# One decoder block on one core: a hand-written order around the MoE routing gets more dummy matmuls ahead, fewer within, an index list earlier and four low parts ahead of other work

## The chip, the cores and the metric

The kernel runs on one core of one Trainium2 chip. The metric is the device time of one execution in microseconds (us); the median of several runs counts. The engines are PE (TensorE: matmuls and transposes), DVE (VectorE), ACT (ScalarE), POOL (GpSimd) and SP (SyncE, which issues most loads). Each engine works through its own instructions strictly in the order in which the program lists them; an instruction whose input is late holds up all that stands behind it on its engine. Matmuls whose type is float32 run here in passes: a matmul of float32 with float32 shows as two records in the trace.

## The reference

A post-norm decoder block with 512 tokens of 1024 channels. The part that matters here comes after attention and the linear recurrence:

```python
x = layer_norm(ALPHA * x + (1 + gt_m) * mix, ln1_g, ln1_b)
u = layer_norm(x) * (1 + sc_f) + sh_f
# routing: top-1 of 4 groups, then top-2 of the 4 experts in that group
grp_prob = softmax(u @ w_grp + b_grp)
grp_w, grp_idx = top_k(grp_prob, 1)
top_w, top_idx = top_k(softmax(sel_logits), 2)
top_w = top_w / sum(top_w) * grp_w
# 16 experts of width 512
h = silu(u @ w_e_gate[e]) * (u @ w_e_up[e])
y = y + comb[:, e] * (h @ w_e_down[e])
x = layer_norm(ALPHA * x + (1 + gt_f) * y, ln2_g, ln2_b)
```

## The kernel before

**Tiles.** The 512 tokens are four tiles of 128 (t = 0 to 3). `TAIL` is a list of closures written out by hand; called one after the other, they set the order of PE, ACT, DVE and POOL from the end of attention to the start of the experts. Behind the list the program order of PE and SP stays as it is written, while ACT, DVE and POOL are interleaved by a scheduler at build time.

**Per token tile.** `L[t][0]` to `L[t][4]` are the steps of the output layer norm (the x of tile t is made on DVE at L945; L957, L978, L984, L994 and L998 follow; the last step stores u to DRAM at L999). `RT[t]` transposes x (PE, L1008), `RE[t]` copies the transposes (ACT, L1013), `RL[t]` is the 8 matmuls of the router (PE, L1034) and `RN[t]` turns them into logits (DVE, L1040 and L1041). `SX[t]` scales x on ACT (L1018) and stores it to `x2d` from ACT's DMA queue (L1019).

**The choice.** `R[0]` to `R[4]` choose group, first and second expert on DVE (from L1191), join the choices in the mask `mkb` (L1212) and count positions with small matmuls on PE (L1215 and L1217, then L1225 and L1228). `K(n)` puts n dummy matmuls of the identity on PE (L1123), whose result nobody reads. `KR(name, n)` puts n dummies on PE that read the mask `em` or the first choice (L1131; the first choice is called `oh1` in the code and `e1o` in the trace), so they start when it is there.

**Gathering expert 0's tokens.** `FO` makes one-hot masks, `FM(t)` multiplies them with u of tile t (PE, L1551, 16 records for one tile) and `FX` splits the sums into a high part `x0h` (ACT, L97) and a low part `x0l` (DVE, L98). `IX[p]` makes the list of token numbers for slot block p: one-hot on DVE (L1379 or L1370), 8 matmuls on PE (L1317), a copy on DVE (L1321). `OR, PT, SP_, PP` sort the experts by load; `PP` leaves the positions on DVE (L1571, L1573). `WM` makes the routing weights `wm` from DVE (L1233 to L1252) and two small ACT steps (L1235, L1241).

**Expert weights.** A weight tile `er` (512 KB, loaded by SP at L819) is split into a high part `whi` (ACT, L811) and a low part `wlo` (DVE, L812; the low part of each second tile of four goes to POOL). `pre_split(g)` does that for gate tile g of expert 0. `whi` and `wlo` have four buffers, so a fifth split waits until PE has finished the first tile. A half (gate, up or down) of an expert is four tiles with six matmuls each (L101 whi x high, L102 wlo x high, L103 whi x low). Right behind the list comes expert 0's gate half, then `IX[2]`, then the transposes of `wm` on PE (L1289, with a copy `sT` on ACT at L1291), then expert 0's up half, then the gathered rows of expert 1 (L1409) and its gate half. Later slot blocks hold 64 tokens each; the last ones are the L1418 matmuls (gate and up, in float32 straight from `er`), L1502 and L1400 (transposes), and a down half as above.

Of the kernel before, what the change touches and what calls it, by code (L numbers as in the profile page):

```python
# [19 lines left out]
S = 512  # L20
# [27 lines left out]
def block_kernel(ctx, tc, x, c, w_ada, b_ada, w_in, b_f, conv_w, conv_b, w_rg, b_rg, w_ig, b_ig,  # L48
# [1816 lines left out]
```

## Time and profile before

| what | value |
|---|---|
| median of 3 runs | 655.67 us (652.84, 655.67, 656.31) |
| the profiled execution's own time | 654.58 us |
| its span, first to last instruction | 652.8 us |
| busy: PE, DVE, ACT, POOL | 92%, 69%, 49%, 28% |
| chain that ended last: PE, DMA, DVE, ACT | 62%, 18%, 10%, 5% |
| mean granted TensorE clock | 0.97 |

The profiled execution took 654.58 us, 1.8 us more than its span. PE is busy nearly all the time, so a stretch of the profile in which PE stands idle, or runs at a granted clock under 1, is where a change in order can act. A granted clock of 1 is 2.4 GHz, one of 0.5 is 1.2 GHz; shares in between are windows in which both occurred.

### The profile page before, as it was taken

The page shows a single profiled execution, that of the slowest core. Times are in us where ns is not written, and L with a number is a line of the kernel's source. Part 1 is how long each engine was busy: PE and PEld are TensorE (multiplying, and loading weights), DVE is VectorE, ACT ScalarE, POOL GpSimd, SP SyncE. Part 2 cuts the span into 40 slices and gives each one's busy share as a digit, 9 for nine tenths or more (in the row PEclk, how much of TensorE's full clock was granted, in tenths as well). Part 3 has the DMA queues.
Part 4 walks back from the last instruction along what each step waited for, and adds up shares of the span by engine and source line. Part 5 has one row for each costly group of instructions (what it writes and reads, how often), then busy time and mean ns, then how long its engine had stood idle before and what let it go on. Part 6 is the DMA issues. An engine that isn't in the chain of part 4 may idle for free.

```text
span 652.8 us, 10217 instructions
## 1 busy us (share of the span) xinstructions
PE 600.1 (92%) x3537; PEld 440.2 (67%) x3537; DVE 453.3 (69%) x740; ACT 322.3 (49%) x512; POOL 180.0 (28%) x186
## 2 busy tenths in 40 slices
PE   4798999999999999989899999999999899999990
PEld 0455877777886888879677776676667577766550
DVE  6757869845744677787798576938686785895264
ACT  0344797344436364644577454445545464753150
POOL 8800002100000000142155353435354343743000
PEclk9899999999999999997899999999999899999996
DMA  9996136996347305375799979799989999999523
GB/s 311 340 266 201 36 117 196 283 276 199 115 166 285 113 4 191 110 278 197 234 332 380 389 233 349 271 328 350 359 285 346 367 377 363 370 385 368 151 104 124
DMA packets 90862, 165.65 MB, mean 254 GB/s; under 512 B 9351, under 2 KB 29943, under 8 KB 90808
## 3 DMA queue, kind: packets, MB, share of 16 engines
q1 hardware_dynamic: 84080, 150.06, 66.2%
q0 software_dynamic: 5024, 10.70, 6.3%
q10 hardware_dynamic: 1704, 4.21, 1.8%
q8 instruction: 29, 0.48, 0.3%
q14 instruction: 25, 0.20, 0.1%
HBM read 156.58 MB, written 12.39 MB: 259 GB/s over the span
## 4 chain that ended last, share of the span: by engine, by line
PE 62%; DMA 18%; DVE 10%; ACT 5%; issue 3%; ACTq 0%; POOL 0%; SPq 0%; POOLq 0%; DVEq 0%
PE ps L101 12%; PE ps L102 12%; PE ps L103 12%; PE ps L1418 7%; DMA er<-in_w_e_up_dram 6%; DMA er<-in_w_e_down_dram 4%; DMA er<-in_w_e_gate_dram 4%; DVE wlo L812 3%; PE ps L1434 2%; DMA wa<-in_w_ada_dram 2%; PE ps L290 2%; DMA wi<-in_w_in_dram 1%; PE ps L318 1%; ACT pr L861 1%; PE ps L883 1%
## 5 line engine op out<-in xcount | busy, mean ns | idle before, releaser
L812 DVE TENSOR_TENSOR wlo<-er,whi 128x1024 fp32r<-128x1024 f32 x91 | 143.9, 1600 | 28.8 <-ACT whi L811 27.1
L811 ACT CAST whi<-er 128x1024 fp32r<-128x1024 f32 x120 | 125.3, 1049 | 73.7 <-PE ps L103 67.0
L812 POOL TENSOR_TENSOR wlo<-er,whi 128x1024 fp32r<-128x1024 f32 x29 | 74.8, 2579 | 76.8 <-ACT whi L811 76.6
L101 PE MATMUL ps<-uh,whi 128*128 128x512 f32 x160 | 64.4, 403 | 0.0
L102 PE MATMUL ps<-wlo,xth 128*128 128x512 f32 x144 | 58.1, 403 | 5.1 <-POOL wlo L812 4.1
L103 PE MATMUL ps<-uh,wlo 128*128 128x512 f32 x160 | 62.6, 392 | 0.0
L102 PE MATMUL ps<-ul,whi 128*128 128x512 f32 x160 | 62.5, 390 | 0.0
L101 PE MATMUL ps<-whi,xth 128*128 128x512 f32 x144 | 58.9, 409 | 0.0
L1418 PE MATMUL ps<-er,xT 128*64 128x256 f32 x512 | 58.8, 382 | 0.0
L103 PE MATMUL ps<-whi,xtl 128*128 128x512 f32 x144 | 57.6, 400 | 1.2 <-DVE xtl L98 1.2
L1418 PEld LDWEIGHTS ps<-er,xT 128*64 128x64 f32 x512 | 35.4, 137 | 19.4 <-issue 1.9
L326 POOL TENSOR_TENSOR rA<-rA,nhalf 128x1 f32<-128x1 f32 x4 | 2.2, 549 | 157.0 <-DVE rA L917 157.0
L101 PEld LDWEIGHTS ps<-uh,whi 128*128 128x128 f32 x160 | 30.1, 188 | 11.9 <-issue 3.9
L358 DVE TENSOR_TENSOR wlo<-wi,whi 128x1024 fp32r<-128x1024 f32 x20 | 25.5, 1275 | 16.9 <-ACT whi L357 16.9
L102 PEld LDWEIGHTS ps<-wlo,xth 128*128 128x128 f32 x144 | 27.4, 190 | 12.7 <-POOL wlo L812 5.8
L357 ACT CAST whi<-wi 128x1024 fp32r<-128x1024 f32 x20 | 21.0, 1048 | 29.0 <-DMA wi<-in_w_in_dram 20.6
L102 PE MATMUL ps<-wlo,hth 128*128 128x512 f32 x80 | 32.6, 407 | 2.6 <-DVE wlo L812 2.6
L103 PEld LDWEIGHTS ps<-uh,wlo 128*128 128x128 f32 x160 | 30.0, 188 | 6.9 <-DVE wlo L358 0.5
L102 PEld LDWEIGHTS ps<-ul,whi 128*128 128x128 f32 x160 | 30.1, 188 | 6.5 <-issue 0.5
L101 PE MATMUL ps<-whi,hth 128*128 128x512 f32 x80 | 33.0, 412 | 0.0
L103 PEld LDWEIGHTS ps<-whi,xtl 128*128 128x128 f32 x144 | 27.5, 191 | 7.9 <-DVE xtl L98 1.6
L103 PE MATMUL ps<-whi,htl 128*128 128x512 f32 x80 | 32.2, 403 | 0.0
(414 smaller groups left out, 1248.9 us busy)
## 6 DMA issues: line engine op xcount, KB each, us to landing
er<-in_w_e_gate_dram SPq DMA_DIRECT2D x64, 512.0 KB, 9.6
er<-in_w_e_up_dram SPq DMA_DIRECT2D x64, 512.0 KB, 11.3
er<-in_w_e_down_dram SPq DMA_DIRECT2D x64, 512.0 KB, 10.7
wa<-in_w_ada_dram SPq DMA_DIRECT2D x44, 512.0 KB, 6.2
wi<-in_w_in_dram SPq DMA_DIRECT2D x20, 512.0 KB, 7.3
wo<-in_w_out_dram SPq DMA_DIRECT2D x8, 512.0 KB, 5.1
wa<-in_w_ada_dram ACTq DMA_DIRECT2D x4, 512.0 KB, 12.1
x<-in_x_dram SPq DMA_DIRECT2D x4, 512.0 KB, 6.2
```

Of the source, the lines that this page charges most:

```text
L101: T.matmul(o, l[0], r[0], start=start, stop=False)
L102: T.matmul(o, l[0], r[1], start=False, stop=False)
L103: T.matmul(o, l[1], r[0], start=False, stop=stop)
L290: T.matmul(part_p[j][32 * k:32 * k + 32, :], cb[:, 2 * kh - 2 + k, :], part_q[j][kh - 1 + k // 2][:, k % 2, :], start=kh == 1, stop=kh == 3)
L318: T.matmul(p[:, b:b + 1], part[:, b * 128:(b + 1) * 128], s4 if sel_ is None else sel_, start=True, stop=True)
L357: A.copy(hl[0], r)
L358: V.tensor_sub(hl[1], r, hl[0].bitcast(F32))
L811: A.copy(hl[0], r)
L812: (eng or V).tensor_sub(hl[1], r, hl[0].bitcast(F32))
L861: A.activation(pr[j][:, n, :], lg_[j][:, n, :], AF.Exp, bias=nmx[:, j, n:n + 1], accum_out=ss[:, j, n:n + 1])
L1418: T.matmul(p[64 * h:64 * h + 64, :], xT[:, k, :], ws[w0 + k // 2][:, k % 2, h * 256:(h + 1) * 256], start=k == 0, stop=k == 7)
L1434: T.matmul(py[64 * h:64 * h + 64, :], hT[:, k % 2, (k // 2) * 64:(k // 2) * 64 + 64], ws[8 + k][:, h * 512:(h + 1) * 512], start=k == 0, s ...
```

## The change

Only the list `TAIL` is edited, at its end. Eight dummies are put in front of `RT[0]`; the dummies inside the choice go from 5 and 5 to 3 and 2; `IX[1]` moves from behind `FX` to a place before `FM(0)`; `pre_split(1)`, `(2)` and `(3)` follow `FX` directly, and `WM`, `SX[1]` and `SX[0]` come behind them.

```diff
-        ..., L[0][0], RT[0], RL[1], L[1][2], RE[0], RN[2], L[1][3], L[0][1], RL[0], L[0][2], K(10), SX[3], RN[1], L[0][3], SX[2], RN[0], ahead(3), R[0], KR("em", 5), R[1], KR("oh1", 5), R[2], R[3], FO, L[2][4], R[4], FM(3), IX[0], OR, FM(2), L[1][4], PT, SP_, FM(1), L[0][4], PP, FM(0), pre_split(0), FX, IX[1], pre_split(1), SX[1], SX[0], WM, pre_split(2), pre_split(3),
+        ..., L[0][0], K(8), RT[0], RL[1], L[1][2], RE[0], RN[2], L[1][3], L[0][1], RL[0], L[0][2], K(10), SX[3], RN[1], L[0][3], SX[2], RN[0], ahead(3), R[0], KR("em", 3), R[1], KR("oh1", 2), R[2], R[3], FO, L[2][4], R[4], FM(3), IX[0], OR, FM(2), L[1][4], PT, SP_, FM(1), L[0][4], PP, IX[1], FM(0), pre_split(0), FX, pre_split(1), pre_split(2), pre_split(3), WM, SX[1], SX[0],
```

On DVE, before, the end of the routing weights (L1252, `wm`) stands ahead of the low parts of expert 0's third and fourth gate tile and of all of its up tiles (`wlo_3238` and `wlo_3242` are those gate tiles, `wlo_3299`, `wlo_3319` and `wlo_3329` are up tiles 0, 2 and 3):

```order
L1249 TENSOR_TENSOR wm_3232<-e1o_3047,wk_3228 128x64
L1251 TENSOR_TENSOR w_665_3234<-e2o_3064,wk_3229 128x64
L1252 TENSOR_TENSOR wm_3232<-wm_3232,w_665_3234 128x64
L812 TENSOR_TENSOR wlo_3238<-er_2324,whi_3237 128x1024
L812 TENSOR_TENSOR wlo_3242<-er_2326,whi_3241 128x1024
L812 TENSOR_TENSOR wlo_3299<-er_2328,whi_3298 128x1024
L812 TENSOR_TENSOR wlo_3319<-er_2739,whi_3318 128x1024
L1321 TENSOR_SCALAR c_3283<-ps_3273 128x1
L812 TENSOR_TENSOR wlo_3329<-er_2741,whi_3328 128x1024
```

In the changed kernel the last rows up to `wm` on DVE are these (`wlo_3323` and `wlo_3333` are the low parts of up tiles 2 and 3; the low parts of the gate tiles and of up tile 0 stand ahead of these rows):

```order
L812 TENSOR_TENSOR wlo_3323<-er_2739,whi_3322 128x1024
L1243 TENSOR_SCALAR den_3233<-dd_3230 128x4
L1321 TENSOR_SCALAR c_3287<-ps_3277 128x1
L1244 TENSOR_TENSOR den_3233<-den_3233,gw_3228 128x4
L1350 CAST ix_3286<-c_3287 128x1
L1351 SCALAR_TENSOR_TENSOR ix_3286<-c_3287,half 128x1
L1246 RECIPROCAL wk_3236<-den_3233 128x4
L1247 TENSOR_TENSOR wk_3237<-wk_3236,dd_3230 128x4
L1249 TENSOR_TENSOR wm_3240<-e1o_3054,wk_3236 128x64
L1251 TENSOR_TENSOR w_670_3242<-e2o_3068,wk_3237 128x64
L812 TENSOR_TENSOR wlo_3333<-er_2741,whi_3332 128x1024
L1252 TENSOR_TENSOR wm_3240<-wm_3240,w_670_3242 128x64
```

The finished weights now stand behind the low part of up tile 3.

On ACT, before, the two stores of x stand behind the cast of gate tile 1 (`whi_3208`), ahead of the other casts:

```order
L811 CAST whi_3208<-er_2322 128x1024
L1018 ACTIVATE xt_1731<-xt_1731 128x1024
L1019 DMA x2d<-xt_1731 128x1024
L1018 ACTIVATE xt_1730<-xt_1730 128x1024
L1019 DMA x2d<-xt_1730 128x1024
L1235 ACTIVATE gx_3218<-gd_3216 128x16
L1241 ACTIVATE dd_3222<-dd_3222 128x4
L811 CAST whi_3237<-er_2324 128x1024
```

In the changed kernel the stretch of ACT that follows the casts of gate tiles 1 to 3 reads as follows (`whi_3302`, `whi_3312`, `whi_3322`, `whi_3332` are up tiles 0 to 3, `sT_3299` the copy of the transposed weights):

```order
L811 CAST whi_3302<-er_2328 128x1024
L811 CAST whi_3312<-er_2737 128x1024
L1235 ACTIVATE gx_3226<-gd_3224 128x16
L811 CAST whi_3322<-er_2739 128x1024
L1241 ACTIVATE dd_3230<-dd_3230 128x4
L1018 ACTIVATE xt_1731<-xt_1731 128x1024
L811 CAST whi_3332<-er_2741 128x1024
L1019 DMA x2d<-xt_1731 128x1024
L1018 ACTIVATE xt_1730<-xt_1730 128x1024
L1291 COPY sT_3299<-ps_3294 16x512
L1019 DMA x2d<-xt_1730 128x1024
```

Both stores, and the two ACT steps of the weights, now stand behind casts of up tiles, and the second store behind `sT`.

Near the end of the kernel the scheduler's interleaving comes out differently too. On ACT, before, the casts of the last down half (`whi_6123` to `whi_6153`, tiles 0 to 3) stand like this around the split of its input (`hth`), the silu of the next block (`sg`) and a copy of transposes (`xT`):

```order
L811 CAST whi_6123<-er_5845 128x1024
L811 CAST whi_6133<-er_5847 128x1024
L811 CAST whi_6143<-er_5849 128x1024
L97 CAST hth_6089<-ps_6084 128x512
L811 CAST whi_6153<-er_5851 128x1024
L1489 ACTIVATE sg_6169<-ps_6067 128x256
L1401 COPY xT_6110<-ps_6111 128x512
```

And in the changed kernel (`whi_6127` to `whi_6157` are the same four tiles):

```order
L97 CAST hth_6093<-ps_6088 128x512
L1489 ACTIVATE sg_6173<-ps_6071 128x256
L811 CAST whi_6127<-er_5849 128x1024
L1401 COPY xT_6114<-ps_6115 128x512
L811 CAST whi_6137<-er_5851 128x1024
L811 CAST whi_6147<-er_5853 128x1024
L811 CAST whi_6157<-er_5855 128x1024
```

Three of the four casts have moved behind `xT`. DVE's low parts of these tiles moved likewise, behind `htl` (L98) and `sg` (L1490).

## Rows read from the trace of the kernel before

**Rows 1.** Chain that ended last, end of the kernel: start, us, engine or transfer.
```profile
609.28 5.15 DMA x2d<-y,ix
```

**Rows 2.** Busy time by windows: window, length, busy us, PEclk, DMA share, GB/s.
```profile
295.00:300.00 5.00, 5.00 (x25) 5.00 (x25) 4.82 (x13) 3.83 (x7) 2.15 (x4) 0.50 0.49 161
320.00:325.00 5.00, 4.94 (x21) 3.69 (x21) 3.31 (x15) 3.41 (x6) 1.70 (x1) 0.66 0.58 190
375.00:425.00 50.00, 48.83 (x299) 33.04 (x299) 39.14 (x43) 24.95 (x29) 22.80 (x12) 1.00 0.83 284
```

**Rows 3.** Timeline of PE, routing: start, us, instruction [idle before <-releaser].
```profile
292.50 1.72 PE L1008 MATMUL ps<-ident,xt 128*128 128x128 f32 x8 [2.19 <-DVE xt L945]
294.01 6.85 PE L1034 MATMUL ps<-wr,yT 128*128 128x20 f32 x32
300.70 3.82 PE L1123 MATMUL ps<-ident 128*128 128x128 f32 x20
304.45 1.31 PE L1131 MATMUL ps<-ident,em 128*64 128x128 f32 x10
...
306.78 0.21 PE L1215 MATMUL ps<-mkb,utrib 128*128 128x16 bf16 x2
...
316.01 2.05 PE L1551 MATMUL ps<-oh,u 128*128 128x128 f32 x16
320.06 0.35 PE L1317 MATMUL ps<-cidx,oh 128*128 128x1 bf16 x8 [2.00 <-DVE oh L1379]
```

**Rows 4.** Timeline of DVE, routing.
```profile
298.68 1.41 DVE L994 SCALAR_TENSOR_TENSOR u<-xt,nmu,scf 128x512 f32<-128x512 f32 x2
300.90 0.24 DVE L1040 SCALAR_TENSOR_TENSOR lg<-ps,rs,b1w 128x20 f32<-128x20 f32 x1 [0.81 <-PE ps L1034]
...
305.64 0.22 DVE L1212 TENSOR_TENSOR mkb<-e1o,e2o 128x64 bf16<-128x64 f32 x1
...
316.12 0.21 DVE L1571 CAST posb<-ps 128x56 bf16<-128x56 f32 x1 [1.48 <-PE ps L1297]
...
319.32 0.68 DVE L1379 TENSOR_TENSOR oh<-iota1b,posb 128x512 bf16<-128x512 bf16 x1
```

**Rows 5.** Timeline of PE, expert 0 and the start of expert 1.
```profile
326.19 0.50 PE L102 MATMUL ps<-wlo,x0h 128*128 128x512 f32 x1 [1.04 <-DVE wlo L812]
...
328.62 0.40 PE L103 MATMUL ps<-whi,x0l 128*128 128x512 f32 x1
...
329.08 0.60 PE L1289 MATMUL ps<-ident,wm 128*16 128x128 f32 x4
...
339.38 0.50 PE L103 MATMUL ps<-whi,xtl 128*128 128x512 f32 x1 [1.20 <-DVE xtl L98]
```

**Rows 6.** Timeline of DVE, the same stretch.
```profile
324.77 0.22 DVE L1252 TENSOR_TENSOR wm<-wm,w 128x64 f32<-128x64 f32 x1
...
328.75 2.99 DVE L812 TENSOR_TENSOR wlo<-er,whi 128x1024 fp32r<-128x1024 f32 x1 [0.34 <-ACT whi L811]
...
331.74 1.21 DVE L812 TENSOR_TENSOR wlo<-er,whi 128x1024 fp32r<-128x1024 f32 x1
```

**Rows 7.** Timeline of POOL, the same stretch.
```profile
327.52 3.14 POOL L812 TENSOR_TENSOR wlo<-er,whi 128x1024 fp32r<-128x1024 f32 x1 [4.73 <-ACT whi L811]
```

**Rows 8.** Timeline of ACT, the same stretch.
```profile
322.08 0.81 ACTq L1019 DMA_DIRECT2D x2d<-xt  x1
...
329.06 1.05 ACT L811 CAST whi<-er 128x1024 fp32r<-128x1024 f32 x1 [0.34 <-PE ps L103]
```

**Rows 9.** Waits of SP's DMA queue: total us, times, longest us.
```profile
SPq L819 <- DMA x2d<-xt: 18.1, 4, 8.7
```

**Rows 10.** Timeline of ACT, last down half.
```profile
592.66 1.05 ACT L811 CAST whi<-er 128x1024 fp32r<-128x1024 f32 x1 [0.30 <-PE ps L103]
...
602.47 0.59 ACT L1401 COPY xT<-ps 128x512 f32<-128x512 f32 x1 [2.42 <-PE ps L1400]
```

**Rows 11.** Timeline of PE, last down half.
```profile
607.82 0.40 PE L103 MATMUL ps<-whi,htl 128*128 128x512 f32 x1
```

More of the change, by code (lines that the diff above doesn't have):

```diff
@@ L42, in TAIL @@
     return [
-        AL, AL, pj(1, 0), AC, AC, AL, AL, pj(1, 1), AC, AC, T[0], S[1], N[1], AU[6], pj(2, 0), LW["L"], AL, GW("L", 0, V), GW("L", 1, V), FW["L"][0], pj(2, 1), AL, T[1], PV[0], S[2], AU[7], N[2], AC, AC, FW["L"][1], GW("L", 2, V), AL, pj(3, 0), AU[8], FW["L"][2], GW("L", 3, V), AL, pj(3, 1), AC, AC, AU[9], open_e1, T[2], S[3], N[3], PV[1], S[4], FW["L"][3], AL, AL, AL, AL, PV[2], T[3], N[4], RW[0], lo(0, 1), AC, AC, PV[3], LW["A"], scsh_rows, FR[0], FR[1], XA[0], XA[2], lo(0, 0), AC, AC, GW("A", 0, V), lo(1, 0), FR[2], le(0, 0), le(0, 1), XA[1], S[5], T[4], N[5], GW("A", 1, V), S[6], lo(2, 1), PV[4], RW[1], FR[3], FR[4], lo(2, 0), GW("A", 2, V), GW("A", 3, V), le(1, 0), AU[10], lo(1, 1), FR[5], le(1, 1), XA[3], S[7], T[5], N[6], SS[3], le(2, 1), S[8], PV[5], lo(3, 0), T[6], N[7], le(2, 0), AU[11], lo(3, 1), FW["A"][0], FW["A"][1], FW["A"][2], FW["A"][3], le(3, 0), T[7], E5, N[8], PV[6], S[9], le(3, 1), oh(3, 0), oh(3, 1), T[8], oe(3, 0), PV[7], N[9], S[10], T[9], N[10], PV[8], oe(3, 1), SS[2], oh(2, 1), oh(2, 0), L[3][0], T[10], RT[3], oe(2, 0), RE[3], PV[9], L[3][1], PV[10], RL[3], SS[1], oe(2, 1), open_e3, ahead(4), oh(1, 0), L[3][2], L[2][0], SS[0], RT[2], RE[2], L[3][3], L[2][1], oh(1, 1), oe(1, 0), oe(1, 1), L[2][2], L[1][0], RN[3], L[3][4], oh(0, 0), RT[1], RE[1], L[1][1], L[2][3], oh(0, 1), RL[2], oe(0, 0), oe(0, 1), L[0][0], RT[0], RL[1], L[1][2], RE[0], RN[2], L[1][3], L[0][1], RL[0], L[0][2], K(10), SX[3], RN[1], L[0][3], SX[2], RN[0], ahead(3), R[0], KR("em", 5), R[1], KR("oh1", 5), R[2], R[3], FO, L[2][4], R[4], FM(3), IX[0], OR, FM(2), L[1][4], PT, SP_, FM(1), L[0][4], PP, FM(0), pre_split(0), FX, IX[1], pre_split(1), SX[1], SX[0], WM, pre_split(2), pre_split(3),
@@ new lines, in TAIL @@
+        AL, AL, pj(1, 0), AC, AC, AL, AL, pj(1, 1), AC, AC, T[0], S[1], N[1], AU[6], pj(2, 0), LW["L"], AL, GW("L", 0, V), GW("L", 1, V), FW["L"][0], pj(2, 1), AL, T[1], PV[0], S[2], AU[7], N[2], AC, AC, FW["L"][1], GW("L", 2, V), AL, pj(3, 0), AU[8], FW["L"][2], GW("L", 3, V), AL, pj(3, 1), AC, AC, AU[9], open_e1, T[2], S[3], N[3], PV[1], S[4], FW["L"][3], AL, AL, AL, AL, PV[2], T[3], N[4], RW[0], lo(0, 1), AC, AC, PV[3], LW["A"], scsh_rows, FR[0], FR[1], XA[0], XA[2], lo(0, 0), AC, AC, GW("A", 0, V), lo(1, 0), FR[2], le(0, 0), le(0, 1), XA[1], S[5], T[4], N[5], GW("A", 1, V), S[6], lo(2, 1), PV[4], RW[1], FR[3], FR[4], lo(2, 0), GW("A", 2, V), GW("A", 3, V), le(1, 0), AU[10], lo(1, 1), FR[5], le(1, 1), XA[3], S[7], T[5], N[6], SS[3], le(2, 1), S[8], PV[5], lo(3, 0), T[6], N[7], le(2, 0), AU[11], lo(3, 1), FW["A"][0], FW["A"][1], FW["A"][2], FW["A"][3], le(3, 0), T[7], E5, N[8], PV[6], S[9], le(3, 1), oh(3, 0), oh(3, 1), T[8], oe(3, 0), PV[7], N[9], S[10], T[9], N[10], PV[8], oe(3, 1), SS[2], oh(2, 1), oh(2, 0), L[3][0], T[10], RT[3], oe(2, 0), RE[3], PV[9], L[3][1], PV[10], RL[3], SS[1], oe(2, 1), open_e3, ahead(4), oh(1, 0), L[3][2], L[2][0], SS[0], RT[2], RE[2], L[3][3], L[2][1], oh(1, 1), oe(1, 0), oe(1, 1), L[2][2], L[1][0], RN[3], L[3][4], oh(0, 0), RT[1], RE[1], L[1][1], L[2][3], oh(0, 1), RL[2], oe(0, 0), oe(0, 1), L[0][0], K(8), RT[0], RL[1], L[1][2], RE[0], RN[2], L[1][3], L[0][1], RL[0], L[0][2], K(10), SX[3], RN[1], L[0][3], SX[2], RN[0], ahead(3), R[0], KR("em", 3), R[1], KR("oh1", 2), R[2], R[3], FO, L[2][4], R[4], FM(3), IX[0], OR, FM(2), L[1][4], PT, SP_, FM(1), L[0][4], PP, IX[1], FM(0), pre_split(0), FX, pre_split(1), pre_split(2), pre_split(3), WM, SX[1], SX[0],
```

## The prediction

> **What bounds the kernel now.** I read the chain of work that ended last first. Its end runs from the last down half over the addition of y into `x2d` [rows 1] to the last layer norm, so a delay of the last down half is a delay of the end. The windows come second: between 375 and 425 us PE is busy 48.83 of 50 us at a granted clock of 1, with the DMA engines at a share of 0.83 [rows 2]. There PE sets the pace, so a shift of PE at expert 1 is carried on. The windows also show two stretches in which the granted clock was near or at the lower of its two levels (1.2 GHz, 2.4 GHz): 0.50 in 295 to 300 and 0.66 in 320 to 325 [rows 2]. Third, the timeline of PE shows what came just before each: PE had stood idle 2.19 us for DVE's x of tile 0, and 2.00 us for the one-hot of the second index list [rows 3]. The change goes at these two waits. Fourth, the timelines of DVE, POOL and ACT around expert 0 say who is late when the order changes there.
>
> **The change part by part.** The sum is made against the profiled execution's own 654.58 us, which lies 1.1 us under the median of the three runs.
>
> *Dummies in front of the last transposes.* K(8) is 16 records. The 20 of K(10) took 3.82 us, most of it at the lower clock [rows 3], 0.19 each; 16 would be 3.0 us at that level and about 1.5 at twice the clock. They lie in the wait of 2.19 us, so they can delay the transposes by 0.8 us at most, and at full clock not at all. If the clock then holds, the 32 router matmuls need about 3.4 us in place of 6.85 [rows 3], and are done near 299. DVE is busy with u of tile 2 until 298.68 + 1.41 = 300.09 and waits 0.81 us more for them today [rows 4]. Only this 0.8 us is won; the rest of the faster matmuls is hidden behind DVE.
>
> *Fewer dummies in the choice.* `mkb` is there at 305.64 + 0.22 = 305.86, yet its first matmul starts at 306.78 [rows 3, 4], because the 20 records of the dummies are not through. Ten of them took 1.31 us, so ten fewer save more than the 0.92 us of lateness, and PE then waits for `mkb`: about 0.86 us won. Together with the first edit the products start 1.66 us earlier, near 305.1. The price could be the clock: K(10) at full clock ends near 301.2, and PE then has three short waits until 305.1, with only 10 records between them. No row shows whether the clock stays up through that. I take nothing, and as the upper bound the loss of a fall like that of 320 to 325, (1 - 0.66) x 5 = 1.7 us [rows 2].
>
> *Second index list earlier.* DVE's wait of 1.48 us ends at 316.12 [rows 4] with the positions, when PE has just finished what made them. Two casts and a one-hot of 0.68 us later, near 317.1, the list's products could start; so PE now stands about 1.05 us in front of FM(0), which itself starts at 316.01 today [rows 3]. Then come 0.3 us of list products and 2.05 us of FM(0): 316.01 + 1.05 + 0.3 + 2.05 - 1.66 = 317.75 for expert 0's first matmul. Today it stands 0.2 us behind 320.06 [rows 3]: 2.5 us won, and the wait of 2.00 us behind which the clock fell is gone.
>
> *Low parts first.* Today a matmul of gate tile 2 waits 1.04 us for its low part [rows 5]. Eleven matmuls between 326.19 and 328.62 start 0.24 us apart [rows 5], so 24 need 5.8 us at full clock. The new order gets the low parts of tiles 1 to 3 behind `x0l` and a one-hot, 1.21 us each [rows 6]; the last near 322.8. The gate half ends near 324.3 (323.5 if DVE never held it) in place of 328.9: 4.5 us won up to here.
>
> *The weights behind the low parts.* This gives it back. The transposes of `wm` stand on PE between gate and up half. Today `wm` is ready at 324.77 + 0.22, four us before PE takes it at 329.08 [rows 5, 6]. In the new order `wm` on DVE stands behind the low part of up tile 3. Its cast reuses the buffer of gate tile 3, and today it starts 0.34 us behind the last gate matmul [rows 8]. So `wm` cannot be there before 0.34 + 1.05 (cast) + 1.21 (low part) + 0.22 = 2.8 us after the gate half's end, whatever DVE does. PE, and with it every matmul of the up half, stands behind these transposes. More is added by POOL: it works on up tile 1 for 3.14 us, until 330.66, and DVE's low part of up tile 2, begun at 328.75, took 2.99 in place of 1.21 us and ended 1.08 us after POOL [rows 6, 7]. In the new order the same pair meets: POOL near 323.0 to 326.1, DVE's low part of tile 2 done at 327.2, nine small steps (1.3 us), the low part of tile 3 at 329.7, `wm` at 329.9. PE waits 5.5 us, and the up half starts near 330.3 in place of 329.4: +0.9.
>
> Rows 6 and 7 show one such meeting. The Trainium skill, page "SBUF — State Buffer", section "Who interferes with whom", makes a rule of it: a VectorE instruction with two inputs in SBUF and a GpSimd instruction that reads SBUF exclude each other, and whichever issues second is blocked until the first is through. The trace agrees (1.08 us after POOL's end is about what is left of an operation of 1.21 us). By the rule the wait is 5.5 us; by DVE's own durations alone (low part of tile 2 at 325.5, `wm` at 328.3) it would be 3.9, and the sum 1.6 us lower.
>
> A wait of 5.5 us is longer than both waits behind which the clock fell. I take the loss of the second fall again, 1.7 us [rows 2], now in the up half; the bounds are 0 and 2.1 (today's whole up half has 24 matmuls, and a longer fall would cost little more).
>
> *What comes back.* Expert 1 waits 1.20 us for its `xtl` today [rows 5], since DVE is behind with low parts; with PE later and DVE done it falls away: -1.2. So expert 0 and 1 together: +0.9 + 1.7 - 1.2 = +1.4 us.
>
> *Stores of x.* The second store issues today at 322.08 [rows 8]; SP's weight loads wait for such stores to land, up to 8.7 us [rows 9]. In the new order it stands behind `sT`, which needs the transposes of `wm`: near 331.3, some 9 us later, and the loads behind it on SP's queue with it. What hides it: the tiles concerned are for expert 1 and later, and in 375 to 425 the DMA engines have 0.17 x 50 = 8.5 us free [rows 2] to catch up. I take 0; the cover is thin, and without it I allow 3 us.
>
> *The end.* The last down half's casts of tiles 0 to 2 are made ahead of time today, the third at 592.66 [rows 10]. Now three stand behind the copy `xT`, which ran at 602.47 [rows 10] and cannot run earlier, since it waits for PE. Tile 1's cast ends near 604.0, its low part on POOL (about 2.6 to 3.1 us) near 606.9, and DVE's low parts of tiles 2 and 3 follow, the first blocked as above, at 607.9 and 609.0. The half then ends near 610.7 in place of 608.2 [rows 11]: +2.5 us, on the chain's end [rows 1]. Bounds: 0 if the casts slip earlier than I read, 4.2 if the clock falls in the wait for tile 1.
>
> **Sum.** 1.4 + 0 + 2.5 = +3.9 us: 658.5 against the profiled execution, and on the median of the runs 655.67 + 3.9 = 659.6. I say 659.5.
>
> **Rivals.**
> - *Half of the loss does not come* (0.28). The clock holds in the up half, or the last casts are hidden. For it: each is seen in no row yet. Then +1.4 to +2.2, about 657.5.
> - *The dummies do not hold the clock* (0.08). For it: K(8) ends before DVE's x is there, if it runs at full clock. Then the 0.8 us of the first edit is gone: 660.4.
> - *Loads late* (0.10). SP's loads are 9 us later against 8.5 us of slack: +3, 662.6.
> - *Faster: the wait for `wm` stays at its floor* (0.12). Place: the transposes between gate and up half. If POOL and DVE don't meet, and the gate half ends at 323.5, the up half starts at 323.5 + 2.8 + 0.35 = 326.7, 2.7 us earlier than today, at full clock, and with the 1.2 us of expert 1 the result is -3.9: 651.8. It decides from a wait under about 3.4 us, and needs the end not to lose. Against it: the order of DVE, with nine steps and a low part between the meeting and `wm`.
>
> **How the numbers follow.** My forecast, both losses, has 0.42. A difference of 0.5%, 3.3 us, is about what a measurement of this kernel can tell from none: slower means above 659.0. The forecast's own range is 658 to 662.5 (the clock at the choice, 1.7, on top); some 0.3 of its 0.42 lies above 659.0, with the two cases above it some 0.48. Same takes the first rival, the rest of the forecast and a little of the last: 0.41. Faster: 0.11. The range goes from 652.5, near the faster case, to 663.0, the late loads.
>
> **What would show it.** Right: no idle of 2 us in front of tile 0's transposes that leads to a clock of 0.5; the products near 305; expert 0's first matmul near 318; an idle time of some 5 us in front of the transposes of `wm`, released by DVE's L1252, with a lower clock behind it; a wait of POOL's low part in the last down half. Wrong: `wm` released within 3 us of the gate half's end; the last down half still ending 8 us behind its transposes' start, 602; or waits of PE for weight loads between 350 and 400 us, which would be the late stores.

## The result and the profile after

| | before | changed |
|---|---|---|
| median of 20 runs each, us | 652.93 | 657.06 |
| ratio (95% interval) | 1 | 1.0065 (1.0048 to 1.0082) |
| span of the profiled execution, us | 652.8 | 657.5 |
| mean granted TensorE clock | 0.970 | 0.972 |

The change makes the kernel 0.65% slower, about 4.2 us. That is the side and nearly the size that was forecast (+3.9); the forecast time, 659.5 us, is 2.4 us too high, because the kernel before measured 652.93 us over 20 runs and not the 655.67 of the first three. The routing first. This is the timeline of PE in the changed kernel, from the last transposes to expert 1's gathered rows:

```profile
292.62 1.33 PE L1008 MATMUL ps<-ident,xt 128*128 128x128 f32 x8 [0.30 <-DVE xt L945]
...
296.94 3.60 PE L1034 MATMUL ps<-wr,yT 128*128 128x20 f32 x16 [1.29 <-ACT yT L1013]
300.37 4.62 PE L1123 MATMUL ps<-ident 128*128 128x128 f32 x20
304.91 1.51 PE L1131 MATMUL ps<-ident,em 128*64 128x128 f32 x6
...
306.79 0.21 PE L1215 MATMUL ps<-mkb,utrib 128*128 128x16 bf16 x2
...
317.13 0.35 PE L1317 MATMUL ps<-cidx,oh 128*128 128x1 bf16 x8 [1.04 <-DVE oh L1379]
...
319.16 0.50 PE L101 MATMUL ps<-whi,x0h 128*128 128x512 f32 x1
...
322.51 0.51 PE L102 MATMUL ps<-wlo,x0h 128*128 128x512 f32 x1 [1.01 <-DVE wlo L812]
...
326.58 0.35 PE L1317 MATMUL ps<-cidx,oh 128*128 128x1 bf16 x8
331.75 1.02 PE L1289 MATMUL ps<-ident,wm 128*16 128x128 f32 x4 [4.82 <-DVE wm L1252]
332.43 0.78 PE L101 MATMUL ps<-whi,x0h 128*128 128x512 f32 x1
333.00 0.63 PE L102 MATMUL ps<-wlo,x0h 128*128 128x512 f32 x1
...
340.17 1.04 PE L1409 MATMUL ps<-ident,xg 128*128 128x128 f32 x8
```

The wait of 2.19 us in front of the transposes is down to 0.30 [rows 3], but a new one of 1.29 us stands in front of the last router matmuls, the dummies behind them are slow, and the positions start at 306.79, as before (306.78). The wait of 2.00 us for the second list [rows 3] is one of 1.04 now. The gate half of expert 0 ends near 326.6, 2.3 us earlier, though it waits 1.01 us for a low part. Then the new wait: 4.82 us for `wm`. The first matmuls of the up half that follows take 0.63 us each and start 0.43 us apart (near its end 0.39 and 0.23), and it ends 5.1 us later than before, where the gathered rows of expert 1 started here:

```profile
335.09 1.04 PE L1409 MATMUL ps<-ident,xg 128*128 128x128 f32 x8
```

Windows of the changed kernel; the third column from the end is the granted clock:

```profile
295.00:300.00 5.00, 3.71 (x21) 3.61 (x20) 4.82 (x14) 3.71 (x7) 2.13 (x5) 0.60 0.47 145
300.00:305.00 5.00, 5.00 (x24) 4.78 (x24) 3.98 (x19) 1.73 (x2) 0.81 (x2) 0.50 0.91 300
315.00:325.00 10.00, 7.95 (x51) 6.20 (x51) 8.06 (x15) 5.98 (x8) 2.58 (x2) 1.00 0.46 136
330.00:350.00 20.00, 18.25 (x105) 14.72 (x106) 12.30 (x24) 13.47 (x16) 8.46 (x5) 0.83 0.82 286
```

The fall of the clock in 320 to 325 [rows 2] is gone. The one of 295 to 300 begins later (0.60) and lasts through the choice (0.50 in 300 to 305), and a new one lies in the up half (0.83 over 330 to 350).

Why `wm` is late is read from three more timelines of the changed kernel. DVE:

```profile
325.94 2.24 DVE L1240 TENSOR_TENSOR dd<-m,m 128x4 f32<-128x4 f32 x1
328.11 1.21 DVE L812 TENSOR_TENSOR wlo<-er,whi 128x1024 fp32r<-128x1024 f32 x1
...
330.34 1.22 DVE L812 TENSOR_TENSOR wlo<-er,whi 128x1024 fp32r<-128x1024 f32 x1
331.48 0.22 DVE L1252 TENSOR_TENSOR wm<-wm,w 128x64 f32<-128x64 f32 x1
```

POOL:

```profile
325.11 3.06 POOL L812 TENSOR_TENSOR wlo<-er,whi 128x1024 fp32r<-128x1024 f32 x1 [1.67 <-ACT whi L811]
```

ACT:

```profile
328.22 0.21 ACT L1241 ACTIVATE dd<-dd 128x4 f32<-128x4 f32 x1 [1.74 <-DVE dd L1240]
...
329.28 1.03 ACT L811 CAST whi<-er 128x1024 fp32r<-128x1024 f32 x1
...
332.88 0.33 ACTq L1019 DMA_DIRECT2D x2d<-xt  x1
```

POOL works on up tile 1 until 328.17. The step that DVE issues meanwhile is not the low part of up tile 2, as in [rows 6], but `dd`, four numbers per partition: 2.24 us, until 328.18. In the kernel before it ran beside no work of POOL:

```profile
323.27 0.15 DVE L1240 TENSOR_TENSOR dd<-m,m 128x4 f32<-128x4 f32 x1
```

ACT's exponential waits 1.74 us for it, the first store's scaling (L1018, 1.04 us) and then the cast of up tile 3 stand behind that on ACT, its low part and `wm` behind that on DVE. What the scaling alone adds to the wait no run here separates: the experiments below move weights and stores together, or (v6) the transposes of `wm` as well.

The last big down half. PE and then ACT of the changed kernel:

```profile
604.03 0.71 PE L1400 MATMUL ps<-ident,xg 64*128 64x64 f32 x8
...
605.82 0.50 PE L102 MATMUL ps<-wlo,hth 128*128 128x512 f32 x1 [0.66 <-DVE wlo L812]
...
608.81 0.50 PE L102 MATMUL ps<-wlo,hth 128*128 128x512 f32 x1 [1.31 <-POOL wlo L812]
...
616.57 0.44 PE L1425 MATMUL ps<-ident,sg 128*128 128x128 f32 x2
```

```profile
604.77 0.59 ACT L1401 COPY xT<-ps 128x512 f32<-128x512 f32 x1 [2.44 <-PE ps L1400]
605.25 2.94 ACT L811 CAST whi<-er 128x1024 fp32r<-128x1024 f32 x3
```

Three casts run only behind `xT` (before, all four were done ahead of it, the third at 592.66 [rows 10]). PE waits 0.66 and 1.31 us for low parts, and the half ends 2.5 us later after its transposes: from these to the next L1425 it is 616.57 - 604.03 = 12.54 us, and 611.75 - 601.73 = 10.02 in the kernel before:

```profile
601.73 0.71 PE L1400 MATMUL ps<-ident,xg 64*128 64x64 f32 x8
...
611.75 0.44 PE L1425 MATMUL ps<-ident,sg 128*128 128x128 f32 x2
```

For the comparison of all kernels I cut each trace by starts of PE's rows: **a** from tile 0's last transposes (L1008) to the positions (L1215), **b** from there to expert 1's gathered rows (L1409), **c** from there to the transposes behind expert 1's gate half (L1502), **mid** from there to the transposes ahead of the last big down half (L1400), **d** from there to the next L1425. For the changed kernel a = 306.79 - 292.62 = 14.17, b = 340.17 - 306.79 = 33.38, d = 616.57 - 604.03 = 12.54. The names of the runs are explained below.

| run | a | b | c | mid | d | ratio to before (95%) |
|---|---|---|---|---|---|---|
| before | 14.28 | 28.31 | 9.83 | 256.81 | 10.02 | |
| changed | 14.17 | 33.38 | 8.38 | 255.48 | 12.54 | 1.0065 (1.0048 to 1.0082) |
| e1 weights back | 13.03 | 29.60 | 9.97 | 253.94 | 10.02 | 1.0014 (0.9985 to 1.0043) |
| e2 index only | 14.53 | 31.86 | 9.12 | 252.13 | 10.02 | 1.0084 (1.0056 to 1.0113) |
| e3 dummies only | 12.99 | 28.05 | 11.15 | 253.48 | 10.02 | 0.9990 (0.9968 to 1.0011) |
| e4 low parts only | 14.27 | 33.98 | 8.38 | 255.62 | 12.53 | 1.0068 (1.0041 to 1.0095) |
| v7 last half on DVE | 12.97 | 33.09 | 8.35 | 252.65 | 11.34 | 1.0030 (0.9998 to 1.0063) |
| v3 wait filled | 12.95 | 31.10 | 9.03 | 253.55 | 10.02 | 1.0032 (1.0001 to 1.0062) |
| v1 transposes late | 13.02 | 26.57 | 12.71 | 255.27 | 14.37 | 1.0060 (1.0023 to 1.0097) |
| v6 and stores first | 13.03 | 30.42 | 15.09 | 254.99 | 10.02 | 1.0068 (1.0035 to 1.0101) |
| n7 weights in the gap | 12.98 | 27.84 | 11.25 | 254.04 | 10.02 | 0.9993 (0.9970 to 1.0015) |
| n8 weights split | 12.97 | 26.73 | 9.73 | 252.24 | 10.02 | 0.9969 (0.9945 to 0.9992) |
| n9 and clock | 12.99 | 27.64 | 11.29 | 251.80 | 10.02 | 0.9969 (0.9946 to 0.9991) |
| n10 late index | 12.98 | 27.23 | 9.14 | 252.23 | 10.02 | 0.9931 (0.9901 to 0.9960) |

One execution of n8 took 1181.89 us and is left out of its ratio. The column "mid", in which no order on PE differs, tells how far one execution may be trusted: it varies by 5.0 us. The windows say why. The kernel before has a lower clock in two windows there:

```profile
500.00:525.00 25.00, 22.25 (x104) 15.92 (x105) 18.37 (x21) 13.01 (x15) 12.06 (x7) 0.93 1.05 366
525.00:550.00 25.00, 23.91 (x148) 17.27 (x146) 17.75 (x17) 12.72 (x15) 11.38 (x6) 0.93 1.04 374
```

The last kernel of the table, n10, has it in neither:

```profile
500.00:525.00 25.00, 23.62 (x120) 17.19 (x119) 20.48 (x21) 15.72 (x20) 13.04 (x7) 1.00 1.04 362
525.00:550.00 25.00, 23.91 (x161) 17.34 (x160) 17.38 (x22) 12.65 (x15) 9.83 (x5) 1.00 1.04 359
```

The changed kernel and e4 have the first fall and not the second (255.5 and 255.6), e1, e3, v3 and n7 the second and not the first (253.5 to 254.0; v1 and v6, which enter the stretch with another backlog, 255.3 and 255.0), and those with neither (e2, v7, n8, n9, n10) need 251.8 to 252.7. In v7 and the changed kernel the order of every engine is the same up to the last big down half; one has the first fall and the other doesn't, so such a fall can differ from one execution to the next. How much of it belongs to a program, one trace of each doesn't tell. So the stages a to d are read from the traces, and the total from the ratio of many runs.

### The profile page after: what moved, and what is told of

The parts are those of the page before. It is cut to its first block, busy times and chain, and to the rows that moved or that the text cites. A ratio compares the mean times of both kernels' runs of the same rounds, so it can differ in the third digit from the quotient of the medians.

```text
span 657.5 us, 10226 instructions
## 1 busy us (share of the span) xinstructions
PE 600.9 (91%) x3543; PEld 440.0 (67%) x3543; DVE 456.5 (69%) x740; ACT 322.0 (49%) x512; POOL 177.1 (27%) x186
## 4 chain that ended last, share of the span: by engine, by line
PE 67%; DMA 10%; DVE 10%; issue 5%; ACT 4%; POOL 2%; ACTq 0%; SPq 0%; POOLq 0%; DVEq 0%
PE ps L102 14%; PE ps L101 14%; PE ps L103 13%; PE ps L1418 6%; PE ps L1434 3%; DMA wa<-in_w_ada_dram 3%; DVE wlo L812 3%; DMA er<-in_w_e_up_dram 2%; DMA er<-in_w_e_down_dram 2%; DMA er<-in_w_e_gate_dram 2%; PE ps L290 2%; DMA wi<-in_w_in_dram 1%; PE ps L1551 1%; POOL wlo L812 1%; ACT pr L861 1%
## 5 line engine op out<-in xcount | busy, mean ns | idle before, releaser
L358 DVE TENSOR_TENSOR wlo<-wi,whi 128x1024 fp32r<-128x1024 f32 x20 | 25.5, 1277 | 18.1 <-ACT whi L357 18.1
L357 ACT CAST whi<-wi 128x1024 fp32r<-128x1024 f32 x20 | 21.0, 1048 | 30.4 <-DMA wi<-in_w_in_dram 22.0
```

The source lines that it names most:

```text
L357: A.copy(hl[0], r)
L358: V.tensor_sub(hl[1], r, hl[0].bitcast(F32))
```

## The experiments

**One part at a time: e1 to e4.** The parts of the list that differ ("..." marks a cut); all else is as in the kernel before (e2 to e4) or the changed one (e1):

```diff
# e1_weights_back: changed kernel, but
-PP, IX[1], FM(0), pre_split(0), FX, pre_split(1), pre_split(2), pre_split(3), WM, SX[1], SX[0],
+PP, IX[1], FM(0), pre_split(0), FX, pre_split(1), SX[1], SX[0], WM, pre_split(2), pre_split(3),
# e2_index_only: kernel before, but
-PP, FM(0), pre_split(0), FX, IX[1], pre_split(1), SX[1], SX[0], WM, pre_split(2), pre_split(3),
+PP, IX[1], FM(0), pre_split(0), FX, pre_split(1), SX[1], SX[0], WM, pre_split(2), pre_split(3),
# e3_dummies_only: kernel before, but
-L[0][0], RT[0], ... R[0], KR("em", 5), R[1], KR("oh1", 5),
+L[0][0], K(8), RT[0], ... R[0], KR("em", 3), R[1], KR("oh1", 2),
# e4_low_parts_only: kernel before, but
-FX, IX[1], pre_split(1), SX[1], SX[0], WM, pre_split(2), pre_split(3),
+FX, IX[1], pre_split(1), pre_split(2), pre_split(3), WM, SX[1], SX[0],
```

> The changed kernel with the routing weights and the stores of x back in front of the low parts of gate tiles 2 and 3; the dummies and the earlier index list stay. Theory: the loss sits in the low parts that stand ahead of the weights, once by the wait for wm (and the lower clock behind it), once by the casts near the end that the scheduler then orders otherwise. Then the transposes of wm start without an idle time, the granted clock is 1 in expert 0, the last down half ends as early after its transposes as before, and the earlier index list is left as a gain of 1.5 to 2.5 us: ratio to before about 0.997. Rival one, the dummies cost: then it stays 2 us or more slower than before. Rival two, the late stores cost: then the gain comes with loads that are 8 us earlier, and the waits of PE between 350 and 600 us change, which the alignment of the two traces there shows.

> The kernel before with only the second index list moved in front of the last one-hot products. Theory: PE waits about 1.05 us in front of them in place of 2.00 us behind them, expert 0 starts 1.1 us earlier and its gate half runs at a granted clock of 1: 1.5 to 2.5 us faster, ratio 0.997. If the dummies matter for this gain, it is smaller here than with them. Rival: the clock falls behind the wait of 1.05 us as well, then the gain is under 0.5 us.

> The kernel before with only the dummies changed (8 in front of the last transposes, 3 and 2 in place of 5 and 5 in the choice). Theory, from the trace of the changed kernel: the fall of the clock only moves from the transposes to the wait of 1.29 us for the last copies, so the ten dummies behind the router matmuls run at the lower clock and the positions start when they did: within 0.5 us of before, ratio 1.000. Rival, as predicted: 1.66 us are won at the positions, ratio 0.9975.

> The kernel before with only the low parts of gate tiles 1 to 3 moved ahead of the weights and the stores. Theory: it has the whole loss and not the gain of the index list: the wait for wm, 4 to 5 us in place of none, against 1 us saved in the gate half, a lower clock in the up half (about 1.8 us), 1.2 us given back at expert 1, and 2.5 us at the last down half: 5 to 7 us slower, ratio 1.009. Rival: without the earlier index list the gate half is late enough for the weights to be ready, then it is within 2.5 us of before.

*Low parts.* e4 has the whole loss: ratio 1.0068, b and d as in the changed kernel. With the weights and stores back in front (e1) d is 10.02 again, b has lost 3.8 of its 5.1 us, and the total is not told apart from that of before (1.0014). This settles where the loss sits, not what part of it the stores have. The rest of b in e1, +1.3 us, goes with the index list below.

*Dummies.* e3 wins 1.3 us in stage a, and so do ten of the eleven traces with the eight dummies in front; only the changed kernel's own profiled execution (14.17) does not. My expectation, drawn from that one trace, said "nothing"; the rival was nearer. The total of e3 is 0.999, not told apart from no change; in its trace the 1.3 us are lost again at expert 1 (c is 11.15 in place of 9.83, at a granted clock of 0.66 in 335 to 340).

*Index list.* Here I was wrong. In the order of before it makes b longer, alone by 3.5 us (e2), and beside the dummies by 1.5 us (e1 against e3); with c it is 2.8 and 0.4 us. Only with the low parts first is b 0.6 us shorter (the changed kernel against e4). e2 is 0.84% slower. PE of e2:

```profile
321.10 0.35 PE L1317 MATMUL ps<-cidx,oh 128*128 128x1 bf16 x8 [1.04 <-DVE oh L1379]
321.31 3.22 PE L1551 MATMUL ps<-oh,u 128*128 128x128 f32 x16
327.67 0.51 PE L102 MATMUL ps<-wlo,x0h 128*128 128x512 f32 x1 [1.02 <-DVE wlo L812]
330.63 0.50 PE L101 MATMUL ps<-whi,x0h 128*128 128x512 f32 x1 [1.54 <-ACT whi L811]
332.18 0.80 PE L102 MATMUL ps<-wlo,x0h 128*128 128x512 f32 x1 [1.04 <-DVE wlo L812]
```

The last one-hot products now stand behind the wait of 1.04 us, and behind it the clock fell here: they took 3.22 in place of 2.05 us. With them come later the split of the sums on ACT and, behind it on ACT in the order of before, two stores and the casts of tiles 2 and 3. The gate half then waits for casts and low parts (1.02, 1.54, 1.04 us), against one wait of 1.04 us in the kernel before [rows 5]; what PE no longer waits in front of the list, it waits there. What e2 loses in total, 3.7 to 7.4 us by its interval, is more than b and c show (+2.8). Its trace is also 3.7 us late ahead of the edit, where every engine's order is that of before, so the rest stays open.

**The end: v7.** Only one instruction changes its engine.

```diff
-                hl = e_split(wq[p][8 + k], G if k in PG else None)
+                hl = e_split(wq[p][8 + k], G if k in PG and p != 9 else None)
```

> The changed kernel with the low part of tile 1 of the last big down half (slot block 9) made by DVE in place of POOL; every other instruction is in the same place. Theory: half of the 2.5 us lost there is POOL's slow low part, which starts late because its cast stands behind the copy of the transposes: the wait of 1.31 us for POOL goes, the half ends 1.2 to 1.3 us nearer to its transposes, the rest of the loss (the low part of tile 0, 0.66 us, and the late casts) stays. Ratio to before 1.004 to 1.005 in place of 1.0065. Rival: the casts alone set the end of this half, then it stays within 0.3 us.

Stage d went from 12.54 to 11.34 us, 1.20 us less, as expected: half of the loss at the end is POOL's late low part. (The ratio, 1.0030, is under the 1.004 to 1.005 that I had expected; its interval takes that range in.) v3 below shows the rest: there the scheduler leaves the cast of tile 1 ahead of `xT` too, only those of tiles 2 and 3 behind it, and d is 10.02, as before.

**The wait and its clock: v3.**

```diff
             IX[2]()
+            K(18)()
             wmT = by_expert(wm)
```

> The changed kernel with 18 dummies on PE (36 records) between the gate half of expert 0 and the transposes of wm, where PE waits 4.8 us. Theory: the wait itself stays, but the granted clock does not fall behind it: the 24 matmuls of the up half start 0.24 us apart from the first on, and the up half ends 1.8 to 2.1 us earlier than in the changed kernel, counted from wm. The scheduler also puts the cast of tile 1 of the last big down half ahead of the copy here, so up to 1.5 us of the loss there may go as well. Ratio to before 1.002 to 1.004. Rival: the dummies delay the transposes by what they win (they are not through when wm is there), then the up half starts later and nothing is won there.

PE of v3:

```profile
326.40 4.26 PE L1123 MATMUL ps<-ident 128*128 128x128 f32 x36
331.48 0.60 PE L1289 MATMUL ps<-ident,wm 128*16 128x128 f32 x4 [0.81 <-DVE wm L1252]
337.51 1.03 PE L1409 MATMUL ps<-ident,xg 128*128 128x128 f32 x8
```

`wm` comes when it came, but the transposes and the up half take 6.03 us in place of 8.42 (340.17 - 331.75). The kernel before took 6.01 us (335.09 - 329.08). So the clock was 2.4 us of the loss in b in the changed kernel's trace; I had taken 1.7 from the windows. It differs by execution: v7, with the same order up to there, took 7.40 us for the same stretch, that is 1.4 us for the clock, and e4 8.77 (340.44 - 331.67), 2.8 us. Transposes and end of the stretch in v7:

```profile
332.06 1.02 PE L1289 MATMUL ps<-ident,wm 128*16 128x128 f32 x4 [4.85 <-DVE wm L1252]
...
339.46 0.71 PE L1409 MATMUL ps<-ident,xg 128*128 128x128 f32 x5
```

**Taking the wait away: v1 and v6.** In both the transposes of `wm` are moved on PE behind the up half; in v6 the stores stand ahead of the weights as well.

```diff
             IX[2]()
-            wmT = by_expert(wm)
...
             xT = e_xt(nxt, gs[nxt])
         if n == 0:
+            wmT = by_expert(wm)
             wb = weight_parts(by_position(wmT))
# v6_stores_first_late, besides
-pre_split(3), WM, SX[1], SX[0],
+pre_split(3), SX[1], SX[0], WM,
```

> The changed kernel with the transposes of wm moved on PE from in front of expert 0's up half to behind it (behind the gathered rows of expert 1). Theory: nothing on PE waits for wm any more; the up half starts as soon as its low parts are there, the wait of 4.8 us shrinks to 1 to 2 us and the clock stays up: the start of expert 1 comes 4 to 6 us earlier than in the changed kernel, that is 0 to 1 us earlier than before. The end keeps its loss of 2.5 us (its casts stand as late as in the changed kernel, one of them later): ratio to before 1.002 to 1.004. Rival: the low parts themselves, not wm, hold the up half (DVE and POOL exclude each other there); then less than 2 us of the 5 comes back.

> As the run with the late transposes, and the two stores of x stand ahead of the weights again (behind the low parts). In this order the scheduler leaves the casts of the last big down half where they were in the kernel before. Theory: both losses are gone and the gain of the gate half stays (2.3 us at its end): expert 1 starts 1 to 2.5 us earlier than before, the last down half ends as early after its transposes as before, ratio to before 0.996 to 0.998. Rival: the late stores or the low parts on DVE eat the gain, then it is within 0.5 us of before.

In v1 b falls from 33.4 to 26.6 us, more than I had said; but the copies, index lists and low parts that waited with `wm` now meet expert 1 (c 12.7 in place of 8.4), and the scheduler's order at the end gets worse still (d 14.4: all four casts behind `xT`, and behind the waits matmuls of 0.63 us, the lower clock). The total is the changed kernel's. In v6 d is back to 10.02, but b is 30.4 and c 15.1, and the total did not move. PE, DVE and POOL of v6, where the up half waits:

```profile
330.19 0.51 PE L102 MATMUL ps<-wlo,x0h 128*128 128x512 f32 x1 [2.53 <-POOL wlo L812]
```

```profile
327.85 2.32 DVE L1243 TENSOR_SCALAR den<-dd 128x4 f32<-128x4 f32 x1
```

```profile
327.61 2.54 POOL L812 TENSOR_TENSOR wlo<-er,whi 128x1024 fp32r<-128x1024 f32 x1
```

A small step of the weights was again shut out by POOL until 330.15. Both expectations failed on the total (v1's interval still reaches into the expected range, v6's does not): among the low parts the work of the weights cost in both of the places in which PE took it up. That it would in any place is not shown.

**The weights out of the way: n7 to n10.** The weights and stores go into a gap of DVE and ACT ahead of the positions of the tokens. n8 splits the weights: both exponentials are issued behind the first one-hot (`WM`), the rest (called `WB` here) in the gap.

```diff
# n7_weights_in_gap: changed kernel, but
-L[0][4], PP, IX[1], FM(0), pre_split(0), FX, pre_split(1), pre_split(2), pre_split(3), WM, SX[1], SX[0],
+L[0][4], WM, SX[1], SX[0], PP, IX[1], FM(0), pre_split(0), FX, pre_split(1), pre_split(2), pre_split(3),
# n8_weights_split: n7, but
-R[3], FO, L[2][4], ... L[0][4], WM, SX[1], SX[0], PP,
+R[3], FO, WM, L[2][4], ... L[0][4], WB, SX[1], SX[0], PP,
# n9_split_and_clock: n8, but
-L[0][1], RL[0], ... KR("em", 3), R[1], KR("oh1", 2),
+L[0][1], K(6), RL[0], ... KR("em", 5), R[1], KR("oh1", 5),
# n10_split_late_index: n8, but
-PP, IX[1], FM(0), pre_split(0), FX, pre_split(1),
+PP, FM(0), pre_split(0), FX, IX[1], pre_split(1),
```

> The changed kernel with the routing weights and then the two stores of x moved ahead of the positions (behind the last step of tile 0's layer norm), where DVE waits 1.48 us for PE and ACT is idle from 314.4 to 318.5. Theory: wm is there long before PE's transposes, so the wait of 4.8 us and the lower clock behind it go, the low parts stay first, and the scheduler leaves the last big down half as before. The weights take 2 to 3 us on DVE against a gap of 1.5, so the one-hot of the second list comes 0.5 to 1.5 us later. Expert 1 starts 1 to 2 us earlier than before; ratio to before 0.996 to 0.999. Rival: the gain of the gate half is hidden behind the low parts of the up half (DVE and POOL), then within 0.5 us of before.

> As the run with the weights in the gap, but the two exponentials of the weights are issued before, behind the first one-hot, so that DVE's second part of the weights (eight steps, 1.6 us) meets no wait for ACT. Theory: the one-hot of the second list comes only 0.2 us later than in the changed kernel; ratio 0.994 to 0.997. Rival: as there.

> As the run with the split weights, with 6 more dummies in front of the last router matmuls (where PE waits 1.29 us for ACT's copies in the changed kernel and the clock then falls) and the dummies of the choice back at 5 and 5. Theory: the granted clock stays at 1 from the transposes through the choice, the positions start at 305.5 in place of 306.8 and nothing behind them runs at the lower clock: another 1 to 2 us less than the run with the split weights, ratio 0.992 to 0.996. Rival: the positions are bound by DVE's choice, and 0.3 us is all that comes.

> The run with the split weights, with the second index list back behind the split of the sums: what the earlier list is worth once the weights hold nobody. Theory: the wait of 2.00 us in front of the list comes back and the clock falls behind it, while the wait of 1.04 us in front of the last one-hot products goes; the time from the positions to expert 1's gathered rows, 26.7 us in the run with the split weights, becomes 28 to 29, and the ratio to before 0.999 to 1.001. Rival: DVE's low parts set the gate half's end either way, then that time stays within 0.5 us and the ratio is 0.997.

In n7 the wait for `wm` is gone and d is as before; the one-hot comes 0.6 us later, the clock falls in FM(0) and again at expert 1 (c 11.25), and the total is that of before, as the rival said. In n8 `wm` is ready 1.3 us after DVE's last big step, while PE still works. DVE of n8 (its line numbers are three higher behind L1233):

```profile
313.37 0.23 DVE L1255 TENSOR_TENSOR wm<-wm,w 128x64 f32<-128x64 f32 x1
313.77 0.21 DVE L1574 CAST posb<-ps 128x56 bf16<-128x56 f32 x1 [0.18 <-PE ps L1300]
```

DVE's wait of 1.48 us [rows 4] is nearly filled (0.18 is left), b is 26.7, and the kernel is 0.3% faster than before, as expected. In n9 the clock held through the choice, yet the positions start no earlier (a 12.99): DVE's choice sets them, as the rival said, and the clock fell one place later. At expert 1 it fell too (0.74 in 340 to 345; c is 11.29 against 9.73 in n8), and the two ratios are equal. PE of n9 (lines as in n8):

```profile
298.22 1.96 PE L1034 MATMUL ps<-wr,yT 128*128 128x20 f32 x16
...
306.89 0.21 PE L1215 MATMUL ps<-mkb,utrib 128*128 128x16 bf16 x2 [0.50 <-DVE mkb L1212]
...
308.34 3.68 PE L1554 MATMUL ps<-oh,u 128*128 128x128 f32 x16 [0.77 <-DVE oh L1544]
```

In n10 the list is back where it was, with its wait (2.31 us), and nothing is lost: b is 27.2 us, not the 28 to 29 that I had expected, and b + c is 36.4 us with the list late and 36.5 with it early. n10 is the fastest of all, 0.69% under before; its interval and that of n8 overlap, so the list's place is not told apart by them.

## Why the prediction was right, point by point

- *Both losses.* The wait for `wm`, its place, its length (5.5 forecast, 4.82 measured), the lower clock behind it and the 2.5 us at the last down half (2.52) are in the trace as forecast. e1 against e4 shows that the low parts ahead of weights and stores cause both. For the second loss this holds in this order alone: it comes through the scheduler's order far behind, and in v3 and v6, with the low parts first as well, d is 10.02. The 2.5 us there are made of two waits, for DVE's low part of tile 0 (0.66 us) and POOL's of tile 1 (1.31); my sum had only the casts, POOL's low part and what follows it.
- *The nearness of the number* is in part luck. Stages a to d of the changed kernel's trace add up to +3.5 + 2.5 = +6.0 us, and "mid", which the edit doesn't order, gave 1.3 back in that execution; with a to c from v7 it is +2.0 + 2.5 = +4.5. The median, about +4.2, is taken over 20 executions. Two of my signs did not come: the products started at 306.79 and not near 305, expert 0's first matmul at 319.16 and not near 318.
- *Sum at expert 1.* +1.4 was forecast. The changed kernel's own trace has -0.11 (a) + 5.07 (b) - 1.45 (c) = +3.5; v7, with the same order up to there, has -1.31 + 4.78 - 1.48 = +2.0. The term that was mis-sized in the first of them is the 1.66 us from the dummies: 1.3 in ten traces, 0.1 in this one, where the last router matmuls (3.60 us), the 20 dummies of K(10) (4.62) and those on `em` (1.51) all ran at the lower clock. The clock in the up half is the second: 1.7 forecast, 2.4 in this trace, 1.4 in v7's. I had expected the clock to hold because the wait at the transposes was filled, and overlooked that the faster router matmuls would run into ACT's copies (1.29 us).
- *Second index list.* Of the "2.5 us won", 1.66 are the dummies' and 0.85 the list's. Expert 0's first matmul came 1.1 us earlier (319.16 against 320.27) with the positions where they were, so for the wait itself the step held. What failed is to take it as won: behind it stands the gate half's end, 4.5 us earlier by forecast, 2.3 measured (most of the difference is the dummies' 1.66 again), and in the order of before the low parts and casts took back more than the list gave (e2). What stands behind the delayed one-hot products on ACT was not in my account.
- *Who is shut out.* The rule of the Trainium skill ("SBUF — State Buffer", section "Who interferes with whom") gave the longer wait, and the longer came nearer (4.8 against 5.5 and 3.9). The instruction that POOL shut out was another one than I had named: `dd`, 2.24 us against 0.15 in the kernel before, not the low part of tile 2. So it is in part luck that the transposes started when I had said, counted from the positions: 24.96 us behind them (331.75 - 306.79), against 329.9 - 305.1 = 24.8. The path was DVE's `dd`, two steps on ACT, a cast and a low part, and not two low parts of DVE.
- *The floor of that wait.* I had read 0.34 us [rows 8] as the distance from the last gate matmul to the cast of up tile 2. It is the time that ACT was idle; the cast began at 329.06, 0.04 us behind that matmul's end (328.62 + 0.40). So the floor was 2.5 us and not 2.8, which changes nothing in the sum and makes the faster rival 0.3 us faster.
- *Late stores.* SP's waits for stores grew, and nothing came of it: in the aligned traces PE of the changed kernel is between 3.60 and 3.66 us late at every row from 345 to 490 us. The row of SP's waits in the changed kernel, against 18.1 us [rows 9]:

```profile
SPq L819 <- DMA x2d<-xt: 27.3, 4, 16.1
```

- *The faster rival* was nowhere near: the wait was 4.8 us, not under 3.4. But its two conditions, no wait for `wm` and an unchanged end, are just what n8 and n10 make, and they are faster by 0.3 and 0.7%.

## What to carry to other kernels

Before moving work ahead of a small result, follow that result through the order of each engine that makes it: here ten small steps of DVE and two of ACT, strung among casts and low parts, held PE for 4.8 us, and the lower clock behind the wait cost another 1.4 to 2.8. Put such steps into a gap that the profile shows on their engine (here 1.48 us in front of the positions), with the waits on other engines taken out beforehand. And where a scheduler orders the rest, compare its order at the far end of the program too: 2.5 us of this loss lay 280 us behind the edit.

## What the hardware showed that I had not expected

- A DVE step of four numbers per partition took 2.24 us in place of 0.15 and ended within 0.01 us of a POOL tensor operation that was under way. e4, v7 and v1 show the same (2.24, 2.25 and 2.28 us, within 0.03 us of POOL's end). It is not only the operations with two tensor inputs: a TENSOR_SCALAR with one took 2.32 us and ended with POOL's in v6.
- The same wait is followed by a lower clock in one execution and not in another: behind the wait of 1.04 us in front of FM(0) the products took 2.03 us in the changed kernel, 3.22 in e2, and in v7, whose order is that of the changed kernel there, 2.77. Filling the wait in front of the transposes moved the fall behind the next wait, of 1.29 us, in the changed kernel; filling that one too, in n9, moved it behind a wait of 0.77 us. In v3, which filled most of the wait for `wm`, the granted clock stayed at 1.00 from 310 to 345 us. FM(0) of the changed kernel and of v7:

```profile
317.35 2.03 PE L1551 MATMUL ps<-oh,u 128*128 128x128 f32 x16
```

```profile
316.91 2.77 PE L1551 MATMUL ps<-oh,u 128*128 128x128 f32 x16
```
